# Two blocks of a transformer on one core: small loads on the load queue, their tables made later, joint units held through both halves, first loads in another order

## The chip, the core and the metric

The kernel runs on one core of one Trainium2 chip. A core has TensorE (PE, matrix products), VectorE (DVE), ScalarE (ACT), GpSimd (POOL) and SyncE (SP, which here only starts transfers), a scratchpad that all of them read and write, accumulator banks, and 16 DMA engines that bring data from HBM. Each engine works through its own queue in order and waits where an instruction needs another engine's result. The metric is the device time of one execution, in microseconds.

## What is computed

Two blocks, one after the other, on 256 tokens of width 1024, in float32. The first has a modulated mixer over the tokens x and a context ctx (attention beside a retention that runs in both directions) and a gated FFN; the second has an FFN, a gated recurrence (HGRN) beside a short convolution, cross-attention to a memory mem_2, and another FFN. Of the reference, what the change touches:

```python
mod_x = silu(c) @ w_mod + b_mod              # six vectors of 1024; columns 0 and 1: shift and scale
hx = rms_norm(x, g_pre_mix) * (1 + sc_m) + sh_m       # hc: the same of ctx, with c_ctx
qa, ka, va, qr, kr, vr, gr = split(h @ w_in)          # of hx and of hc
qa, ka = rms_norm(heads(qa), q_norm_g), rms_norm(heads(ka), k_norm_g)
lg = -exp(ret_decay)                         # per head; decays exp(lg * position) in the retention
ret_x = bidir_retention(rope(qr_x), rope(kr_x), vr_x, lg_f, lg_b, states of ctx)
...
z = rms_norm(x) @ w_in_2                     # HGRN f, q, i, g and the convolution's c, u, b
k_mem, v_mem = split(rms_norm(mem_2) @ w_kv_mem_2)
x = x + attention(x @ w_q_mem_2, k_mem, v_mem) @ w_o_mem_2
```

## The kernel before, in words

Products are made from float32 numbers in two parts: a high part `hi` that TensorE multiplies at its fast float32 rate, and the rest `lo`; a product is hi·hi plus hi·lo plus lo·hi (`mm3`). Tokens stand in tiles of 128: A and B of x, C and D of ctx.

Weights come in units of 128 x 1024 floats (512 KB). `Unit.load` (L386) starts the transfer on SyncE's queue into one of four raw buffers. `Unit.prepare` (L408) splits the unit: ScalarE copies the raw buffer to `hi`, VectorE subtracts to get `lo`, each in one of six ring slots, and the raw buffer comes free. `Unit.get` (L421) hands the unit to the matmuls; at the call that brings its count `uses` to 0 the ring slots go back to the list of free ones, and the next split may be written into the program for them. That split then waits on the chip until the last matmul that reads the slot is done.

The program is fixed when it is built. Threads (written as generators, such as `memory`, `projections`, `small_tables`, `joints`) yield what they need next; a planner picks one after the other and puts the loads and splits in between. What it picks sets the order of the instructions on each engine, and each engine keeps to that order on the chip. The loads stand in the sequence that the string `ORDER` (L40) spells: u is a unit of w_kv_mem_2, 0 and 1 are blocks of w_mod for its first two columns (these may lie in ring slots, unsplit), x is a tile of ctx or x (C, D, A, B), k, a, r, y, q, g are units of w_in, o of w_out, m the other blocks of w_mod, f a place in the first FFN.

At the start TensorE multiplies the w_kv_mem units with the normalised memory (`mm<-k,hi` in the trace) and the w_mod blocks with silu(c) (`acc<-...,cwide`) as they come in. When the sixteen blocks of columns 0 and 1 are done, ctx and x are modulated (`xj`) and the k, a, r projections follow.

`keep` holds the identity (its first 128 columns, loaded first of all) and constants: cosines, sines, positions. `small` holds q_norm_g, k_norm_g and the sixteen decays. Both feed `small_tables` (L948): ScalarE makes exp of the decays (`lg`), GpSimd multiplies it with positions (`dec`) and makes tables for the rotation (`rope`), then ScalarE takes the exponential of `dec`.

The joint stage multiplies w_in_2 units of 8 x 128 x 128 with both token tiles at once. `joint` (L1504) takes two units, each in two halves of 12 matmuls with a yield ahead of each half, so that other threads' work can come between. Between them run the level pairs of the recurrence (`hgrn`, L1564): two groups of small matmuls (`mm<-k,k`), whose results VectorE merges into `macc` with masked copies (`COPY_PREDICATED`).

Of the kernel before, what the change touches and what calls it, by code (L numbers as in the profile page):

```python
# [18 lines left out]
P = 128  # L19
# [17 lines left out]
SOFT2 = 4  # L37


ORDER = "1u11xux11ux11ux1u00u00u00u00ukukaaaaururrrymymymmyummmmmqmqmmmmmuqmqggggmmoooomomommmomouufmfmffmfmmfffffm"  # L40


COLS = {}
# [9 lines left out]
ROWS = {}  # L53
# [13 lines left out]
NKEEP = K_POS + 8  # L67
# [199 lines left out]
def blocks_kernel(ctx: ExitStack, tc: tile.TileContext, a, out):  # L267
    nc = tc.nc
    model = Model()
# [5 lines left out]
    def load(queue, out, in_):  # L275

        n = free_size(out) / 1024.0
        run = 4 * in_.shape[-1]
        model.op("dma", (1.21 + 281.0 / run) * n, (out,), (), 2.0)
        queue.dma_start(out=out, in_=in_)  # L280
# [51 lines left out]
    def pacc(shape=(P, 512)):  # L332
        return new(ps, "acc", shape)


    keep = const.tile([P, NKEEP], F32, name="keep")
    cols = const.tile([P, NCOL], F32, name="cols")
    small = const.tile([P, 144], F32, name="small")
# [142 lines left out]
    def w_unit(w, r0, kt, c0, width, uses, kind="split", early=False):  # L481
        src = w[r0:r0 + kt * P, c0:c0 + width].rearrange("(k p) c -> p k c", p=P)
        return Unit((kt, width), [(0, width, src)], uses, kind, early=early)
# [55 lines left out]
    def until(cond):  # L539
        if not cond():  # L540
            yield cond, None
# [98 lines left out]
    w_in2 = a["w_in_2"][0]  # L640
    accs = {}
    done = set()
# [17 lines left out]
    def load_x(t):  # L660
        def consume(u):
            done.add(("x", t))
        i = "ABCD".index(t)
        src = a["x"] if t in "AB" else a["ctx"]
        u = Unit(None, [], 1, consume)

        def load_it():
            x_in[t] = x_res[t] if t in "AB" else k4()
            load(nc.sync, x_in[t], src[0, (i % 2) * P:(i % 2 + 1) * P, :])
            u.there = model.ready(x_in[t])  # L670
        u.load = load_it

    mods = [(j, kt) for j in (2, 3, 4, 5) for kt in range(8)]

    units = {z: [] for z in "u01karyqgo"}

    def first(z):
        i = len(units.get(z, ()))
        if z == "m":
            if mods:  # L680
                mod_unit(*mods.pop(0))
            return
        if z == "x":
            if xs_left:
                load_x(xs_left.pop(0))
            return
        if z == "u":
            u = w_unit(wkv, 0, 8, (D + i * P) % (2 * D), P, 1)
        elif z in "01":
            u = w_unit(w_mod, i * P, 1, int(z) * D, D, 1, "plain", early=True)  # L690
        elif z == "k":
            u = w_unit(w_in, 512 * i, 4, 512, 256, 4)
        elif z == "o":

            u = w_unit(w_out, P * i, 1, 0, D, 2) if i >= 4 else Unit((1, D), [
                (0, D, w_out[64 * h:64 * h + 64, :].unsqueeze(1), slice(64 * g, 64 * g + 64))
                for g, h in enumerate((i, 4 + i))], 2)
        else:
            c0, uses = {"a": (0, 2), "r": (1280, 4), "y": (1792, 4), "q": (768, 2), "g": (2304, 2)}[z]
            u = w_unit(w_in, 256 * i, 2, c0, 512, uses)  # L700
        units[z].append(u)

    xs_left = list("CDAB")
    head, tail = ORDER.split("f", 1)
    for z in head:
# [49 lines left out]
        return Ffn(len(ffns), gu, dn, step)  # L755

    def units2(c0):
        return [[w_unit(w_in2, 0, 8, c0 + 256 * i + P * b, P, 1) for b in range(2)] for i in range(2)]

    f0 = ffn_units([(a["w_ffn_in"][0], 0), (a["w_ffn_in"][0], FF)], a["w_ffn_out"][0], tail)  # L760
    f1 = ffn_units([(a["ffn1_gate_2"][0], 0), (a["ffn1_up_2"][0], 0)], a["ffn1_down_2"][0])
# [12 lines left out]
    for i in range(2):  # L774
        for h in range(2):
            s = slice(h * 512, (h + 1) * 512)
# [9 lines left out]
    xt, xsT = {}, {}  # L786
# [3 lines left out]
    for i in range(2):  # L790
        for b in (0, 1):
            c = slice(i * P, (i + 1) * P)
            split_cols(mh[b][:, :, c], ml[b][:, :, c], "mem_norm_2", t_bank(mem_t[i], 4 * b), 0, 4 * b)

    load(nc.scalar, keep[:, P:NKEEP], a["consts"][:, P:NKEEP])
    o0 = ROWS["q_norm_g"][0]
    load(nc.scalar, small, a["rows"][o0:o0 + 144].partition_broadcast(P))

    def memory():

# [145 lines left out]
    lb = const.tile([P, 3, 4], F32, name="lb")  # L946

    def small_tables():  # L948
        yield (small, keep), None
        act(out=lg, in_=small[:, 128:144], func=ACTF.Exp)  # L950
        pool.tensor_scalar(out=lg, in0=lg, scalar1=-1.0, scalar2=None, op0=ALU.mult)
        for i in range(8):
            half = 0 if i in (0, 1, 4, 5) else 8
            pool.tensor_scalar(out=dec[:, i, :], in0=lg[:, half:half + 8], scalar1=keep[:, K_POS + i:K_POS + i + 1],
                               scalar2=None, op0=ALU.mult)
        e = sm(8)
        l0, l1 = (cols[:, COLS["lb_param_2"] + 4 * i:COLS["lb_param_2"] + 4 * i + 4] for i in range(2))
        dve.tensor_tensor(out=lb[:, 0, :], in0=l0, in1=l1, op=ALU.max)
        dve.tensor_tensor(out=e[:, 0:4], in0=l0, in1=lb[:, 0, :], op=ALU.subtract)
        dve.tensor_tensor(out=e[:, 4:8], in0=l1, in1=lb[:, 0, :], op=ALU.subtract)  # L960
        for i in range(2):
            cos = keep[:, K_COS + 64 * i:K_COS + 64 * i + 64]
            sin = keep[:, K_SIN + 64 * i:K_SIN + 64 * i + 64]
            for q in range(2):
                g = small[:, 64 * q:64 * q + 64]
                pool.tensor_tensor(out=rope[:, q, i, 0, :], in0=cos, in1=g, op=ALU.mult)
                pool.tensor_tensor(out=rope[:, q, i, 1, 0:32], in0=sin[:, 0:32], in1=g[:, 32:64], op=ALU.mult)
                pool.tensor_tensor(out=rope[:, q, i, 1, 32:64], in0=sin[:, 32:64], in1=g[:, 0:32], op=ALU.mult)
            pool.tensor_scalar(out=rope[:, 2, i, 0, :], in0=cos, scalar1=0.125, scalar2=None, op0=ALU.mult)
            pool.tensor_scalar(out=rope[:, 2, i, 1, :], in0=sin, scalar1=0.125, scalar2=None, op0=ALU.mult)  # L970
        yield from until(lambda: "C" in xsT)
        act(out=e, in_=e, func=ACTF.Exp)
        act(out=dec, in_=dec, func=ACTF.Exp)
        dve.tensor_scalar(out=dec[:, 4:8, :], in0=dec[:, 4:8, :], scalar1=0.125, scalar2=None, op0=ALU.mult)
        dve.tensor_tensor(out=lb[:, 2, :], in0=e[:, 0:4], in1=e[:, 4:8], op=ALU.add)
        dve.reciprocal(out=lb[:, 2, :], in_=lb[:, 2, :])
        dve.tensor_tensor(out=lb[:, 0, :], in0=e[:, 0:4], in1=lb[:, 2, :], op=ALU.mult)
        dve.tensor_scalar(out=lb[:, 1, :], in0=lb[:, 0, :], scalar1=-1.0, scalar2=1.0, op0=ALU.mult, op1=ALU.add)
# [525 lines left out]
    def joint(us):  # L1504

        yield "acc", None
        o = pacc((P, 2, 256))
        for b, u in enumerate(us):
            for half in range(2):
                yield xj, u  # L1510
                if half == 0:
                    hi, lo = u.get()
                for k in range(4 * half, 4 * half + 4):
                    mm3(o[:, b, :], hi[:, k, :], lo[:, k, :], xj[0][:, :, k, :], xj[1][:, :, k, :], k == 0, k == 7)
        st["o"] = o
# [257 lines left out]
```

## Time and profile before

| | us |
|---|---|
| median of three runs | 1071.71 (1069.2 to 1075.77) |
| the profiled execution | 1070.85 |
| its span in the trace | 1069.0 |
| TensorE busy | 1015.5 (95%) |
| VectorE busy | 691.3 (65%) |
| ScalarE busy | 517.0 (48%) |
| GpSimd busy | 11.2 (1%) |

Times in the trace count from the start of the span. A row of a timeline has a start, a length, the engine, the line that issued the instruction (L231, L258, L263 and L280 are helpers), the operation with output and input, how many in a row it merges, and in brackets how long the engine stood idle before and on whose result it waited. `PEclk` is the clock granted to TensorE, 1.00 being full speed.

### The profile page before, as it was taken

Reading aid. Unit: us, or ns where it says so; the run is one execution under the profiler, and the core shown is the slowest. Engines: PE = TensorE matmul, PEld = TensorE weight load, DVE = VectorE, ACT = ScalarE, POOL = GpSimd, SP = SyncE. Lnnn points to the kernel's source line nnn. Section 1 sums busy time; section 2 is a strip of 40 time slices with the busy share of each in tenths; the row PEclk is TensorE's granted clock in tenths of the full one; section 3 lists DMA queues with packets and bytes.
Section 4 is the critical chain, followed back from the end, with each engine's and each line's share of the span. In section 5 each row is a group of like instructions: output and inputs, shape, how many; then the busy total and the mean of one; then the engine's idle time right before and its main releaser. Section 6 shows DMA issues by size and latency. Waiting matters only on the chain. (4 is left out here: it accounts for less than half of the span.)

```text
span 1069.0 us, 16569 instructions
## 1 busy us (share of the span) xinstructions
PE 1015.5 (95%) x6506; PEld 891.1 (83%) x6506; DVE 691.3 (65%) x1140; ACT 517.0 (48%) x839; POOL 11.2 (1%) x34
## 2 busy tenths in 40 slices
PE   5989999998899999989999999998999999999996
PEld 3778877876699999968999998798978779999995
DVE  3468777787765655577656665667877476666654
ACT  5665245563654444445444444662245474444433
POOL 3000000000000000000000000000000000000000
PEclk9899999998899999999999999999999999999999
DMA  9863566562476766674566665574335256666641
GB/s 322 280 206 111 184 229 198 148 197 79 138 226 189 239 193 179 202 230 139 177 185 195 190 189 169 153 217 131 111 127 177 61 177 197 192 188 190 180 158 40
DMA packets 196110, 189.58 MB, mean 177 GB/s; under 512 B 6336, under 2 KB 167616, under 8 KB 196032
## 3 DMA queue, kind: packets, MB, share of 16 engines
q1 hardware_dynamic: 194160, 184.12, 56.3%
q10 hardware_dynamic: 1872, 4.41, 1.3%
q8 instruction: 51, 0.84, 0.3%
q14 instruction: 27, 0.22, 0.1%
HBM read 187.45 MB, written 1.05 MB: 176 GB/s over the span
## 5 line engine op out<-in xcount | busy, mean ns | idle before, releaser
L231 DVE TENSOR_TENSOR lo<-raw,hi 128x1024 fp32r<-128x1024 f32 x296 | 357.5, 1223 | 186.7 <-ACT hi L231 185.5
L231 ACT ACTIVATE hi<-raw 128x1024 fp32r<-128x1024 f32 x296 | 307.3, 1055 | 205.7 <-PE acc L258 88.9
L258 PE MATMUL mm<-xj,hi 128*128 128x256 f32 x1728 | 310.1, 282 | 0.0
L258 PEld LDWEIGHTS mm<-xj,hi 128*128 128x128 f32 x1728 | 268.6, 188 | 4.5
L258 PE MATMUL mm<-xj,lo 128*128 128x256 f32 x864 | 243.0, 281 | 0.0
L258 PE MATMUL acc<-hi,kh 128*128 128x512 f32 x528 | 176.4, 395 | 0.8 <-ACT kh L231 0.8
L258 PEld LDWEIGHTS mm<-xj,lo 128*128 128x128 f32 x864 | 162.6, 188 | 0.0
L258 PEld LDWEIGHTS acc<-hi,kh 128*128 128x128 f32 x528 | 99.1, 188 | 22.2 <-ACT kh L231 1.2
L258 PE MATMUL acc<-hi,k 128*128 128x512 f32 (+1 forms) x320 | 103.7, 394 | 4.7 <-DVE k L231 4.3
L258 PE MATMUL acc<-lo,kh 128*128 128x512 f32 x264 | 103.8, 393 | 0.0
L258 PE MATMUL acc<-hi,xj 128*128 128x512 f32 (+1 forms) x288 | 91.6, 389 | 1.7 <-DVE xj L231 1.7
L231 ACT ACTIVATE k<-k 128x256 f32<-128x256 f32 (+3 forms) x50 | 25.5, 510 | 108.4 <-DVE k L231 108.4
L258 PEld LDWEIGHTS acc<-hi,k 128*128 128x128 f32 x320 | 59.9, 191 | 19.5 <-issue 5.6
L258 PE MATMUL mm<-hi,xj 128*128 128x512 f32 x192 | 68.3, 420 | 3.0 <-ACT xj L231 2.7
L258 PEld LDWEIGHTS acc<-hi,xj 128*128 128x128 f32 x288 | 53.1, 188 | 14.5 <-DVE xj L231 2.3
L258 PE MATMUL acc<-lo,k 128*128 128x512 f32 (+1 forms) x160 | 61.6, 385 | 0.0
L263 PE MATMUL tp<-keep,k 128*128 128x128 f32 x288 | 46.8, 291 | 13.3 <-DVE k L231 4.3
L263 PEld LDWEIGHTS tp<-keep,k 128*128 128x128 f32 x288 | 35.3, 148 | 27.6 <-DVE k L231 7.6
L258 PE MATMUL acc<-xj,hi 128*128 128x256 f32 x320 | 58.2, 284 | 0.0
L258 PEld LDWEIGHTS acc<-lo,kh 128*128 128x128 f32 x264 | 49.8, 189 | 9.1
L258 PE MATMUL mm<-k,hi 128*128 128x256 f32 x256 | 52.6, 306 | 3.4 <-ACT hi L231 3.4
L258 PE MATMUL acc<-lo,xj 128*128 128x512 f32 (+1 forms) x144 | 54.9, 381 | 0.0
(161 smaller groups left out, 1152.1 us busy)
## 6 DMA issues: line engine op xcount, KB each, us to landing
raw<-in_w_in_dram SPq DMA_DIRECT2D x50, 512.0 KB, 4.6
raw<-in_ffn_down_dram SPq DMA_DIRECT2D x44, 512.0 KB, 3.7
raw<-in_w_ffn_in_dram SPq DMA_DIRECT2D x36, 512.0 KB, 4.8
raw<-in_ffn_gate_dram SPq DMA_DIRECT2D x36, 512.0 KB, 4.7
raw<-in_ffn_up_dram SPq DMA_DIRECT2D x36, 512.0 KB, 4.8
raw<-in_w_mod_dram SPq DMA_DIRECT2D x35, 512.0 KB, 4.5
raw<-in_w_ffn_out_dram SPq DMA_DIRECT2D x22, 512.0 KB, 4.2
raw<-in_w_kv_mem_dram SPq DMA_DIRECT2D x16, 512.0 KB, 4.9
```

The source lines that it names most:

```text
L231: return f(**kw)
L258: self.pe.matmul(out=out, lhsT=lhsT, rhs=rhs, start=start, stop=stop)
L263: self.pe.transpose(out, in_, ident)
```

## The change

The string ORDER is another one, with a new letter s. The loads of the rest of `keep` (132 KB) and of `small` (72 KB) move from ScalarE's queue, where they stood after the split of mem_2, to SyncE's, where they are a unit of their own (`load_small`) at the place of s. `small_tables` starts once these have been taken up and tile C of ctx has been transposed. Joint units have two uses instead of one and `get` is called for each half, so their ring slots go back after the second.

```diff
-ORDER = "1u11xux11ux11ux1u00u00u00u00ukukaaaaururrrymymymmyummmmmqmqmmmmmuqmqggggmmoooomomommmomouufmfmffmfmmfffffm"
+ORDER = "11uu1xux111usx11xu00u0uu00u00u0uaakakraurrrmyymmmyyummmmmquqmmmmmmgqqomggmgoommoommmomomuoufmfmffmfmmfffffm"
...
+    def load_small():
+        u = Unit(None, [], 1, lambda u: done.add(("x", "small")))
+
+        def load_it():
+            load(nc.sync, keep[:, P:NKEEP], a["consts"][:, P:NKEEP])
+            o0 = ROWS["q_norm_g"][0]
+            load(nc.sync, small, a["rows"][o0:o0 + 144].partition_broadcast(P))
+            u.there = model.ready(small)
+        u.load = load_it
...
+        if z == "s":
+            load_small()
+            return
...
     def units2(c0):
-        return [[w_unit(w_in2, 0, 8, c0 + 256 * i + P * b, P, 1) for b in range(2)] for i in range(2)]
+        return [[w_unit(w_in2, 0, 8, c0 + 256 * i + P * b, P, 2) for b in range(2)] for i in range(2)]
...
-    load(nc.scalar, keep[:, P:NKEEP], a["consts"][:, P:NKEEP])
-    o0 = ROWS["q_norm_g"][0]
-    load(nc.scalar, small, a["rows"][o0:o0 + 144].partition_broadcast(P))
...
     def small_tables():
-        yield (small, keep), None
+        yield from until(lambda: ("x", "small") in done and "C" in xsT)
...
-        yield from until(lambda: "C" in xsT)
         act(out=e, in_=e, func=ACTF.Exp)
         act(out=dec, in_=dec, func=ACTF.Exp)
...
             for half in range(2):
                 yield xj, u
-                if half == 0:
-                    hi, lo = u.get()
+                hi, lo = u.get()
```

In the program, first ScalarE's queue right after the split of mem_2, before (raw_158 and raw_166 are the first two w_kv_mem units, k_1_80 and k_2_81 mem_2, k_16 and k_18 ctx):

```order
L280 DMA keep<-in_consts_dram 128x264 [waits DMAHW2_49]
L280 DMA small<-in_rows_dram 128x144 [waits DMAHW3_49]
L231 ACT_TABLE_LOAD
L231 ACTIVATE lg<-small 128x16 [waits DMAHW3_49]
L231 ACTIVATE hi_221<-raw_158 128x1024 [waits DMAHW7_49]
L231 ACTIVATE k_37_265,sm_97<-k_1_80 128x1024
L231 ACTIVATE k_38_267,sm_97<-k_2_81 128x1024 [waits DMAHW5_49,DMAHW4_49]
```

and after, where raw_158 and raw_160 are the first two units:

```order
L231 ACTIVATE hi_199<-raw_158 128x1024 [waits DMAHW0_49]
L231 ACTIVATE hi_206<-raw_160 128x1024 [waits DMAHW1_49]
L231 ACTIVATE k_40_239,sm_97<-k_1_80 128x1024 [waits DMAHW3_49,DMAHW2_49]
L231 ACTIVATE k_41_241,sm_97<-k_2_81 128x1024 [waits DMAHW5_49,DMAHW4_49]
L231 ACTIVATE hi_255<-raw_166 128x1024 [waits DMAHW6_49,DMAHW4_49,PE_49]
L231 ACTIVATE k_48_261,sm_183<-k_17_164 128x1024 [waits DMAHW3_49]
L231 ACTIVATE k_49_267,sm_183<-k_19_168 128x1024 [waits DMAHW5_49]
```

Two loads, a table load and lg are gone from ahead of the first split, and the splits of the first two units stand one behind the other.

The same queue further on, around the exponential of dec, before (tp are transposed tiles, vm the memory's values on their way to the scratchpad, raw_225 a w_kv_mem unit):

```order
L231 ACTIVATE k_61_359<-k_18_168,sm_292 128x1024
L231 ACTIVATE sm_193<-sm_193 128x8
L231 ACTIVATE dec<-dec 128x64 [waits Pool_49]
L231 ACTIVATE vm<-tp_373,sm_270 128x128 [waits PE_49]
L231 ACTIVATE vm<-tp_373,sm_270 128x128
L231 ACTIVATE hi_413<-raw_225 128x1024 [waits DMAHW5_49,Activation_49]
```

and after, where raw_204 is the fifth w_kv_mem unit:

```order
L231 ACTIVATE k_65_365<-k_19_168,sm_270 128x1024
L231 ACT_TABLE_LOAD
L231 ACTIVATE lg<-small 128x16 [waits DMAHW3_49]
L231 ACTIVATE sm_378<-sm_378 128x8 [waits DVE_49]
L231 ACTIVATE dec<-dec 128x64 [waits Pool_49]
L231 ACTIVATE vm<-tp_411,sm_244 128x128 [waits PE_49]
L231 ACTIVATE vm<-tp_411,sm_244 128x128
L231 ACTIVATE k_66_367<-tp_451 128x512 [waits PE_49,Activation_49]
L231 ACTIVATE hi_457<-raw_204 128x1024 [waits DMAHW0_49]
```

The table load and lg now stand directly ahead of dec, which waits for GpSimd's work on lg; two copies to vm, one to k and the split of raw_204 follow.

ScalarE's queue in the joint stage, around the load of macc that comes shortly before the first level pair, before (hi<-raw are splits of units, k<-acc copies of joint results):

```order
L231 ACTIVATE hi_7206<-raw_7082 128x1024 [waits DMAHW4_49,DVE_49,PE_49]
L231 ACTIVATE hi_7236<-raw_7112 128x1024 [waits DMAHW5_49,DVE_49,PE_49]
L231 ACTIVATE k_1348_6999<-acc_7193 128x512 [waits PE_49]
L280 DMA macc_7258<-in_consts_dram 128x896
L231 ACTIVATE hi_7276<-raw_7147 128x1024 [waits DMAHW6_49,DVE_49,PE_49]
L231 ACTIVATE hi_7319<-raw_7177 128x1024 [waits DMAHW7_49,DVE_49,PE_49]
L231 ACTIVATE k_1377_7256<-acc_7263 128x512 [waits PE_49]
L231 ACTIVATE hi_7367<-raw_7210 128x1024 [waits DMAHW0_49,DVE_49,PE_49]
```

and after:

```order
L231 ACTIVATE hi_7200<-raw_7076 128x1024 [waits DMAHW3_49,DVE_49]
L231 ACTIVATE hi_7218<-raw_7094 128x1024 [waits DMAHW4_49,DVE_49,PE_49]
L231 ACTIVATE k_1348_6999<-acc_7187 128x512 [waits PE_49]
L231 ACTIVATE hi_7252<-raw_7141 128x1024 [waits DMAHW5_49,DVE_49]
L280 DMA macc_7258<-in_consts_dram 128x896
L231 ACTIVATE hi_7301<-raw_7159 128x1024 [waits DMAHW6_49,DVE_49,PE_49]
L231 ACTIVATE k_1374_7250<-acc_7263 128x512 [waits PE_49]
L231 ACTIVATE hi_7361<-raw_7204 128x1024 [waits DMAHW7_49,DVE_49]
L231 ACTIVATE hi_7379<-raw_7222 128x1024 [waits DMAHW0_49,DVE_49,PE_49]
```

Every split there waited for TensorE (PE) before; now every second one doesn't, among them the one ahead of the load of macc that stands next to the first level pair, and the copies of joint results fall at other places between them.

On SyncE's queue the fifth w_kv_mem load is now followed by two w_mod blocks that go to raw buffers, and five further w_kv_mem loads stand between these and the last w_mod block of columns 0 and 1. On TensorE eight w_kv_mem units and the sixteen blocks stand ahead of the end of the last block before and after; behind it stand two units before and three after, then the k projections. From the first FFN to the joint stage TensorE's order is the same. In VectorE's queue two subtractions instead of one now stand ahead of the masked copies of the third level pair, and one fewer ahead of the last chain of the recurrence.

## Rows read from the trace of the kernel before

**Rows 1.** The page: span, and busy time of each engine.

```profile
span 1069.0 us, 16569 instructions
...
PE 1015.5 (95%) x6506; PEld 891.1 (83%) x6506; DVE 691.3 (65%) x1140; ACT 517.0 (48%) x839; POOL 11.2 (1%) x34
```

**Rows 2.** Stretches: length, busy us (count) per engine, granted clock, DMA share, GB/s.

```profile
0.00:20.00 20.00, 8.75 (x45) 4.58 (x46) 6.02 (x21) 10.21 (x25) 3.35 (x12) 1.00 0.89 307
20.00:40.00 20.00, 17.62 (x120) 15.13 (x120) 8.18 (x29) 10.26 (x20) 5.09 (x20) 0.83 0.98 336
40.00:60.00 20.00, 18.37 (x171) 15.40 (x171) 8.13 (x22) 13.39 (x24) 0.00 (x0) 1.00 0.61 196
100.00:120.00 20.00, 20.00 (x113) 17.36 (x113) 18.01 (x32) 6.16 (x7) 0.00 (x0) 1.00 0.54 175
720.00:740.00 20.00, 17.38 (x146) 17.01 (x145) 13.00 (x17) 5.21 (x6) 0.00 (x0) 1.00 0.48 145
```

**Rows 3.** Timeline of ScalarE at the start: start, us, instruction [idle before <- releaser].

```profile
10.03 0.44 ACTq L280 DMA_DIRECT2D small<-in_rows_dram  x1
...
16.91 0.22 ACT L231 ACTIVATE lg<-small 128x16 f32<-128x16 f32 x1 [4.83 <-DMA small<-in_rows_dram]
17.04 1.04 ACT L231 ACTIVATE hi<-raw 128x1024 fp32r<-128x1024 f32 x1
```

**Rows 4.** Timeline of TensorE at the start.

```profile
12.33 1.08 PE L258 MATMUL acc<-lo,cwide 128*32 128x256 f32 x8 [1.71 <-DMA lo<-in_w_mod_dram]
...
18.13 0.80 PE L258 MATMUL mm<-k,hi 128*128 128x256 f32 x2 [3.43 <-ACT hi L231]
...
27.38 0.58 PE L258 MATMUL mm<-k,lo 128*128 128x256 f32 x1 [2.38 <-DVE lo L231]
```

**Rows 5.** Two stretches: the second w_kv_mem unit, and the k projections.

```profile
24.50:32.40 7.90, 5.52 (x29) 5.32 (x26) 3.92 (x19) 2.09 (x2) 0.59 (x2) 0.64 1.08 356
75.50:91.50 16.00, 13.09 (x99) 11.87 (x98) 13.47 (x33) 11.38 (x27) 0.00 (x0) 1.00 0.35 99
```

**Rows 6.** Timeline of ScalarE, joint stage.

```profile
725.82 1.06 ACT L231 ACTIVATE hi<-raw 128x1024 fp32r<-128x1024 f32 x1 [4.12 <-PE acc L258]
```

**Rows 7.** Timeline of VectorE, joint stage and its end.

```profile
726.91 1.23 DVE L231 TENSOR_TENSOR lo<-raw,hi 128x1024 fp32r<-128x1024 f32 x1 [4.11 <-ACT hi L231]
728.05 1.34 DVE L231 COPY_PREDICATED macc<-keep,mm 128x512 f32<-128x512 uint32 x2
...
775.92 1.23 DVE L231 TENSOR_TENSOR lo<-raw,hi 128x1024 fp32r<-128x1024 f32 x1 [1.82 <-ACT hi L231]
```

**Rows 8.** Timeline of TensorE, joint stage and its end.

```profile
730.64 2.02 PE L258 MATMUL mm<-k,k 128*128 128x128 f32 x16 [1.86 <-DVE k L231]
...
783.09 0.66 PE L263 MATMUL tp<-keep,k 128*128 128x128 f32 x4 [1.32 <-DVE k L231]
```

**Rows 9.** Timeline of GpSimd at the start.

```profile
17.57 3.35 POOL L231 TENSOR_SCALAR dec<-lg,keep 128x8 f32<-128x8 f32 x8
```

**Rows 10.** Timeline of ScalarE, 30 to 40 us.

```profile
35.58 0.24 ACT L231 ACTIVATE dec<-dec 128x64 f32<-128x64 f32 x1
```

**Rows 11.** Timeline of ScalarE at a table load in the joint stage.

```profile
704.13 1.28 ACT L231 ACT_TABLE_LOAD   x1
705.43 0.60 ACT L231 ACTIVATE k<-acc 128x512 f32<-128x512 f32 x1
```

**Rows 12.** Timeline of TensorE, 60 to 95 us.

```profile
64.55 0.64 PE L258 MATMUL acc<-raw,cwide 128*32 128x256 f32 x8
...
78.39 0.51 PE L258 MATMUL acc<-hi,xj 128*128 128x256 f32 x2 [1.11 <-DVE xj L231]
```

**Rows 13.** Timeline of SyncE's queue: issue, us, load.

```profile
3.54 0.43 SPq L280 DMA_DIRECT2D raw<-in_w_kv_mem_dram  x1
...
40.10 0.38 SPq L280 DMA_DIRECT2D raw<-in_w_kv_mem_dram  x1
...
47.82 0.38 SPq L280 DMA_DIRECT2D raw<-in_w_kv_mem_dram  x1
```

## The prediction

> **What bounds the kernel now.** I read the page first, then the table of stretches, then the rows of single engines at the two places that the change touches. TensorE is busy 1015.5 us of a span of 1069.0 [rows 1], so whatever the change brings must come out of 53.5 us in which TensorE stands still, and out of stretches in which it runs below its upper clock. The stretches show where that is [rows 2]: 11.25 us of the first 20 have no matmul, the next 20 lose 2.4 us and run at a granted clock of 0.83, and 720 to 740 us loses 2.6. From 100 to 120 us it is full (20.00 of 20.00); a unit that moves there costs its own length and nothing else.
>
> The start. ScalarE's queue runs in order. It issues the load of `small` at 10.03 us, and then its first exponential waits 4.83 us for it, until 16.91 [rows 3]. Right behind stands the split of the first w_kv_mem unit (17.04, 1.04 us), and TensorE takes up that unit at 18.13 after 3.43 us that the row puts down to this split [rows 4]. The second unit waits another 2.38 us at 27.38 for VectorE's half of its split [rows 4], and the stretch around it has a granted clock of 0.64, a mean between the chip's levels of 1.2 and 2.4 GHz [rows 5].
>
> The joint stage. A joint unit has two halves with a scheduling point between them. In the kernel before its ring slot was handed on after the first, so the next split was queued while the second half still read the slot. The rows show the price: ScalarE stands 4.12 us until 725.82 for TensorE, VectorE's subtraction waits 4.11 us behind that, and the masked copy of the first level pair stands behind it, at 728.05 [rows 6, 7]. TensorE then waits 1.86 us at 730.64 for the chain behind the copy, and 1.32 us at 783.09 for a chain that a subtraction with a wait of 1.82 us delayed [rows 7, 8].
>
> **Part 1, first split no longer behind `small`.** The change takes two DMAs and the exponential out of ScalarE's queue there. The first unit then waits for its own load. In the new order that load is the third large one behind mem_2; in the kernel before the third was the low half of w_mod, for which TensorE waited until 12.33 [rows 4]. With 1.04 us for the split [rows 3] the unit starts at about 13.4 instead of 18.13: **-4.7 us**; bounds -0.9, if only the issue time of two such DMAs (0.44 each) [rows 3] is saved, and -5.8 (18.13 less 12.33).
>
> **Part 2, the second unit's wait.** Its load now stands directly behind the first unit's, and its split directly behind the first split. The 2.38 us should go [rows 4]. Were the stretch also at the upper clock, 5.52 busy us times 0.36 would be another 2.0 [rows 5]. I take **-2.4**, bounds 0 and -4.4; the clock I leave out, because the unit still follows a stretch with little work.
>
> **Part 3, the tables made later.** They now start once ctx C is transposed, which puts four things into ScalarE's busy stretch around 30 us: a table load (1.28 us), the exponential (0.22), and `dec`'s exponential, which waits for GpSimd. From `lg` at 16.91 to the end of GpSimd's `dec` rows, 17.57 plus 3.35, are 4.0 us [rows 3, 9]; in the kernel before `dec`'s exponential came at 35.58, when GpSimd had been done with it for 14.7 us [rows 10]. Now ScalarE stands there for that time less lg's own 0.22, some 3.8 us, and queued behind it are two vm copies, a k copy and the split of raw_204: TensorE waits for the split, and its transposes for the banks that the copies free. Bounds 0 (TensorE has other units in hand) and +5.1 (3.8 plus the table load, all on the path); I take **+2.0**, nearer the middle since two split units are then ahead.
>
> The table load by itself: the row at 704.13 is followed by ScalarE's next instruction at 705.43, 1.30 us later, without a gap [rows 11]. The Trainium skill (ScalarE: Activation LUTs, What ACT_TABLE_LOAD costs) gives about 1.28 us for the load and 1.38 more for a drain, 2.66 in all, for every switch; by that, an estimate from this page, the term would be 1.4 us dearer. The rows decide here: no drain is seen.
>
> **Part 4, the loads in another order.** Up to the last w_mod load of columns 0 and 1 the queue now carries two more units (512 KB each) and the small loads. At the 307 and 336 GB/s of the first two stretches [rows 2] some 17 MB are in by about 56 us, against 64.55 at which TensorE takes the last of these blocks [rows 12]. So bytes are not the limit, as long as SyncE isn't held by raw buffers (a rival). Work before that point is the same, eight w_kv_mem units and sixteen w_mod blocks, so parts 1 to 3 carry over: the last block ends near 60 instead of 65.2. Behind it three units instead of two stand ahead of the k projections. These take 16.00 us, of which TensorE is busy 13.09, with waits such as 1.11 us for VectorE's xj [rows 5, 12]. The third unit fills time of that kind, and is missing later where TensorE is full: **-2.0**, bounds 0 and -2.9. The other moved units (m, y, q, g, o) lie in full stretches; one new wait like the second unit's would cost 2.4: **+0.5**, bounds -0.5 and +2.4.
>
> **Part 5, joint units held through both halves.** The split ahead of the first level pair no longer names TensorE among its waits, so the 1.86 us goes [rows 8]. At the end one subtraction fewer stands ahead of the last chain, so part of the 1.32 goes too. Against that, at the third pair two subtractions stand in a row ahead of the masked copy. I take **-2.5**, bounds 0 and -3.2. Holding the slot longer costs no matmul: the hardware had to wait for the second half in either kernel (the 4.12 us) [rows 6], only what queues behind that wait differs.
>
> **Sum.** -4.7 - 2.4 + 2.0 - 2.0 + 0.5 - 2.5 = -9.1 us. The profiled execution took 1070.85 us (span 1069.0), 0.9 below the median of 1071.71; the sum gives 1061.75 for it and **1062.6** against the median. I write 1062.5.
>
> **Rivals.**
> *The start is bound by its loads.* DMA is at 0.89 and 0.98 in the first two stretches [rows 2]; moving small loads from one queue to another takes no byte away. Then part 1 is worth only its issue time, -0.9, part 2 nothing, and the sum is -0.9 + 2.0 - 2.0 + 0.5 - 2.5 = -2.9: **1069**. For it speaks that share; against it that ScalarE's wait is put down to `small` alone, not to the unit's load issued at 3.54 on the other queue [rows 3, 13]. The Trainium skill (DMA: Bandwidth & Descriptors, Issuing engines are not separate DMA queues) says that DMAs from any engine run on the same 16 DMA engines and interleave, so a second queue saves only the sequencer's time to start them; that is this rival's rule.
>
> *The joint wait only moves*, to the third pair with its two subtractions. Part 5 is then 0 and the sum -6.6: **1065**.
>
> *More than I take.* -4.7 - 4.4 + 0.5 - 2.9 - 3.2 with nothing for moved units, -14.7: **1057**. For it: full clock after an earlier start, and ScalarE's stall covered.
>
> *Slower: raw buffers hold SyncE.* Two w_mod blocks now lie in raw buffers behind raw_204, and five more w_kv_mem loads precede the last w_mod load, each waiting for one of the four buffers. In the kernel before such a cycle took 7.7 us (40.10 to 47.82) [rows 13]. If ScalarE's stall delays the splits, the buffers come free late, and each cycle makes TensorE wait like the second unit did: 2.4 us and 2.0 of clock, 4.4. Without part 2 the sum is -6.7, so from two such waits on it is slower than before, and with four it is +10.9: **1083**. Against it: in the kernel before those cycles show no such wait, since 40 to 60 us is busy 18.37 of 20 [rows 2].
>
> **How the numbers follow.** Chances: forecast 0.47 (1059 to 1066), loads 0.17, joint wait moved 0.10, more 0.18, slower 0.08. One per cent, about what a measurement of this kernel can tell from no change, is 10.7 us: faster by more is under 1061.0, which holds the case "more" and somewhat under half of the forecast, 0.18 + 0.22 = 0.40. Slower by more is the last rival, 0.08; the rest, 0.52, lies within. The range runs from 1055, below "more", to 1071, above the first rival; what is left out is the slower case and the tails of those two.
>
> **What would show it.** Right: the first w_kv_mem matmul at 13 to 14 us; no wait of the second unit; `dec`'s exponential with an idle time of 3 to 4 us put down to GpSimd; the last w_mod block of columns 0 and 1 ending near 60; k projections with under 2 us of idle time; no wait of TensorE before the first level pair, and under 0.7 us before the last chain. Wrong: SyncE rows 7 us apart between 30 and 55, granted clock under 0.8 there, or a wait over 1 us at the third level pair. My weakest term is part 3: whether TensorE has enough split units in hand while ScalarE stands.

## The result and the profile after

The changed kernel takes 1059.53 us (median of four runs, 1055.50 to 1061.01), the kernel before 1072.95 in the same comparison: ratio 0.9871, 95% interval 0.9829 to 0.9913, 13.4 us less. The forecast was 1062.5 us, within 1055 to 1071. In a later comparison the ratio was 0.9884 (0.9851 to 0.9918). A ratio is not formed as the quotient of the two medians, so the two can differ by some tenths of a per cent. The profiled execution took 1061.01 us, its span is 1059.2.

The page of after, to be read beside [rows 1]:

```profile
span 1059.2 us, 16575 instructions
...
PE 1011.6 (96%) x6506; PEld 889.1 (84%) x6506; DVE 691.4 (65%) x1140; ACT 517.8 (49%) x839; POOL 10.6 (1%) x34
```

TensorE's idle time fell from 53.5 to 47.6 us, its busy time by 3.9 (fewer matmuls at the lower clock and after waits). The table of stretches of after, beside [rows 2] and the second of [rows 5]; columns as there:

```profile
0.00:20.00 20.00, 12.01 (x65) 7.89 (x65) 7.57 (x21) 11.01 (x25) 0.66 (x6) 1.00 0.89 291
20.00:40.00 20.00, 18.63 (x174) 14.57 (x171) 10.09 (x38) 13.40 (x25) 7.79 (x25) 1.00 1.00 342
40.00:60.00 20.00, 15.34 (x116) 13.06 (x116) 8.11 (x17) 12.32 (x21) 0.00 (x0) 0.83 0.89 279
74.20:88.90 14.70, 12.98 (x99) 11.94 (x98) 12.07 (x31) 10.41 (x24) 0.00 (x0) 1.00 0.33 98
220.00:240.00 20.00, 19.38 (x127) 16.82 (x126) 15.14 (x33) 8.52 (x25) 0.00 (x0) 0.83 0.46 136
680.00:800.00 120.00, 120.00 (x848) 111.78 (x847) 93.33 (x157) 57.14 (x85) 0.00 (x0) 1.00 0.51 153
```

The first 20 us have 12.01 us of matmuls instead of 8.75, and 20 to 40 us runs at 1.00. But 40 to 60 us, which held 18.37 us before, holds 15.34 at a clock of 0.83. In 680 to 800 us TensorE never stands; before, it was busy 114.97 of the 120:

```profile
680.00:800.00 120.00, 114.97 (x818) 106.19 (x817) 84.91 (x135) 50.92 (x67) 0.00 (x0) 1.00 0.49 146
```

TensorE's timeline of after at the start:

```profile
14.09 0.79 PE L258 MATMUL mm<-k,hi 128*128 128x256 f32 x2 [1.81 <-ACT hi L231]
...
42.67 0.66 PE L263 MATMUL tp<-keep,k 128*128 128x128 f32 x4 [1.18 <-ACT vm L231]
46.80 1.08 PE L258 MATMUL acc<-lo,cwide 128*32 128x256 f32 x8 [3.48 <-DMA lo<-in_w_mod_dram]
...
64.63 0.67 PE L258 MATMUL tp<-k,ones 128*128 128x256 f32 x2 [1.62 <-DVE k L231]
```

The first w_kv_mem unit begins at 14.09 instead of 18.13, and nothing up to 42 us waits as long as the second unit did [rows 4]. Then a w_mod block is late by 3.48 us, and rows of two matmuls behind it, 0.40 long at the upper clock, take 0.63. The last block of columns 0 and 1 ends at 63.0 instead of 65.2, and the tp<-k,ones row behind it, the sums of the table below, starts 2.6 us earlier than this row of before:

```profile
67.24 0.78 PE L258 MATMUL tp<-k,ones 128*128 128x256 f32 x2 [2.05 <-DVE k L231]
```

That is within what profiles of one start differ by: kernels with the start of before have the row at 63.00 to 67.24, those with the start of after at 63.18 to 64.63 (the column of sums below).

ScalarE of after, around the exponential of dec (beside [rows 3, 10]):

```profile
29.98 1.28 ACT L231 ACT_TABLE_LOAD   x1
31.27 0.22 ACT L231 ACTIVATE lg<-small 128x16 f32<-128x16 f32 x1
...
34.27 0.26 ACT L231 ACTIVATE dec<-dec 128x64 f32<-128x64 f32 x1 [2.68 <-POOL dec L231]
...
35.41 1.06 ACT L231 ACTIVATE hi<-raw 128x1024 fp32r<-128x1024 f32 x1
```

It stands 2.68 us for GpSimd, and the split of the fifth unit is the row at 35.41. The Trainium skill's 1.38 us drain beside a table load (ScalarE: Activation LUTs, What ACT_TABLE_LOAD costs) is not there either: the instruction ahead of the load ends at 29.96, and 29.98 to 31.27 is 1.29 us. GpSimd's row (beside [rows 9]), and SyncE's queue (beside [rows 13]):

```profile
31.93 2.31 POOL L231 TENSOR_SCALAR dec<-lg,keep 128x8 f32<-128x8 f32 x8
```

```profile
30.08 2.95 SPq L280 DMA_DIRECT2D hi<-in_w_mod_dram  x1
37.76 1.91 SPq L280 DMA_DIRECT2D raw<-in_w_kv_mem_dram  x2
39.72 0.57 SPq L280 DMA_DIRECT2D lo<-in_w_mod_dram  x1
```

SyncE stands from 33.0 (30.08 plus 2.95) to 37.76, when the raw buffer of the fifth unit is free, and the load issued at 39.72 is the block for which TensorE waits at 46.80. The joint stage in TensorE's timeline, all eight pairs of small matmuls, beside [rows 8], and VectorE at the first of them, beside [rows 7]:

```profile
718.96 1.95 PE L258 MATMUL mm<-k,k 128*128 128x128 f32 x16
...
723.62 1.95 PE L258 MATMUL mm<-k,k 128*128 128x128 f32 x16
...
729.73 1.95 PE L258 MATMUL mm<-k,k 128*128 128x128 f32 x16
...
735.84 1.95 PE L258 MATMUL mm<-k,k 128*128 128x128 f32 x16
...
740.50 1.95 PE L258 MATMUL mm<-k,k 128*128 128x128 f32 x16
...
745.17 1.95 PE L258 MATMUL mm<-k,k 128*128 128x128 f32 x16
...
751.28 1.95 PE L258 MATMUL mm<-k,k 128*128 128x128 f32 x16
...
758.82 1.95 PE L258 MATMUL mm<-k,k 128*128 128x128 f32 x16
```

```profile
719.32 1.23 DVE L231 TENSOR_TENSOR lo<-raw,hi 128x1024 fp32r<-128x1024 f32 x1 [0.52 <-ACT hi L231]
720.46 1.34 DVE L231 COPY_PREDICATED macc<-keep,mm 128x512 f32<-128x512 uint32 x2
```

No pair waits. VectorE's subtraction ahead of the first masked copies waits 0.52 us where it waited 4.11.

### The profile page after: what moved, and what is told of

Read it like the earlier page. It is cut to its first block, busy times and chain, and to the rows that moved or that the text cites. A ratio compares the mean times of both kernels' runs of the same rounds, so it can differ in the third digit from the quotient of the medians.

```text
span 1059.2 us, 16575 instructions
## 1 busy us (share of the span) xinstructions
PE 1011.6 (96%) x6506; PEld 889.1 (84%) x6506; DVE 691.4 (65%) x1140; ACT 517.8 (49%) x839; POOL 10.6 (1%) x34
## 4 chain that ended last, share of the span: by engine, by line
PE 81%; DVE 7%; issue 4%; ACT 4%; DMA 3%; POOL 0%; SPq 0%; ACTq 0%; DVEq 0%; POOLq 0%
PE acc L258 39%; PE mm L258 39%; PE tp L263 3%; ACT k L231 2%; DVE sm L231 2%; DVE k L231 2%; DVE lo L231 2%; ACT hi L231 1%; DVE macc L231 1%; DMA raw<-in_w_ffn_out_dram 1%; DMA row<-in_rows_dram 1%; DMA lo<-in_w_mod_dram 1%; DMA raw<-in_w_in_dram 0%; DMA raw<-in_w_mod_dram 0%; DVE xj L231 0%
## 5 line engine op out<-in xcount | busy, mean ns | idle before, releaser
L231 ACT ACTIVATE hi<-raw 128x1024 fp32r<-128x1024 f32 x296 | 307.0, 1055 | 189.9 <-PE acc L258 65.7
L231 DVE TENSOR_TENSOR k<-k,k 128x256 f32<-128x256 f32 (+4 forms) x79 | 40.7, 524 | 21.6 <-ACT k L231 20.3
```

The costliest lines, as they stand in the source:

```text
L231: return f(**kw)
```

## The experiments

Each kernel is compared with the kernel before; ratios are with their 95% intervals. There were several such comparisons, each with its own runs of before (medians 1071 to 1074), so kernels of two comparisons are set against each other by their ratios, not by their medians. joint_only, no_joint, dec_after_D and after_again are one comparison; order_only, small_only, long_stall and early_lg another; the two hold kernels a third; the two mods_first kernels a fourth. The table gives starts of rows in each profile: the first w_kv_mem matmul, the sums behind the last w_mod block (tp<-k,ones), the first matmul of the first FFN (acc<-hi,kh), the first level pair (mm<-k,k), the product with macc (mm<-k,macc), and the stretch from the pair to macc.

| kernel | median us | ratio | unit 1 | sums | FFN | pair | macc | pair to macc |
|---|---|---|---|---|---|---|---|---|
| before | 1071 to 1074 | 1 | 18.13 | 67.24 | 298.33 | 721.49 | 774.70 | 53.21 |
| after, first profile | 1059.53 | 0.9871 (0.9829 to 0.9913) | 14.09 | 64.63 | 294.97 | 718.96 | 767.26 | 48.30 |
| after_again | 1059.17 | 0.9884 (0.9851 to 0.9918) | 13.31 | 63.57 | 291.39 | 714.99 | 763.25 | 48.26 |
| joint_only | 1064.14 | 0.9938 (0.9913 to 0.9963) | 16.94 | 63.87 | 294.50 | 720.18 | 768.44 | 48.26 |
| hold_beside_pairs | 1065.16 | 0.9943 (0.9915 to 0.9970) | 17.22 | 65.70 | 294.78 | 717.38 | 763.77 | 46.39 |
| hold_f_q | 1071.48 | 1.0015 (0.9988 to 1.0042) | 16.88 | 63.00 | 293.58 | 717.80 | 769.95 | 52.15 |
| no_joint | 1066.24 | 0.9926 (0.9903 to 0.9949) | 13.69 | 63.18 | 291.58 | 715.81 | 770.57 | 54.76 |
| order_only | 1070.60 | 0.9964 (0.9943 to 0.9985) | 18.12 | 63.47 | 302.00 | 726.27 | 779.48 | 53.21 |
| small_only | 1070.33 | 0.9968 (0.9948 to 0.9988) | 13.88 | 60.05 | 296.60 | 721.08 | 775.86 | 54.78 |
| dec_after_D | 1055.97 | 0.9850 (0.9822 to 0.9879) | 13.28 | 59.66 | 289.43 | 715.31 | 763.57 | 48.26 |
| long_stall | 1060.99 | 0.9875 (0.9850 to 0.9900) | 13.23 | 64.97 | 295.44 | 719.16 | 767.42 | 48.26 |
| early_lg | 1054.18 | 0.9819 (0.9794 to 0.9844) | 12.55 | 57.55 | 287.41 | 710.81 | 759.11 | 48.30 |
| mods_first | 1054.46 | 0.9845 (0.9811 to 0.9880) | 12.75 | 59.24 | 290.13 | 714.63 | 762.93 | 48.30 |
| early_lg_mods_first | 1052.96 | 0.9826 (0.9787 to 0.9865) | 13.62 | 57.07 | 284.21 | 711.90 | 760.16 | 48.26 |

A single profile holds the early columns only to some us: four kernels have the start of before (before, joint_only and the two hold kernels), and their FFN begins anywhere from 293.58 to 298.33; the profiled executions of the two hold kernels were the fastest of their 11 and 12. The last column is steadier. So the start is judged by ratios here, the joint stage by both.

**The joint part alone and left out.** joint_only:

```diff
+        ... w_unit(w_in2, 0, 8, c0 + 256 * i + P * b, P, 2) ...
-                if half == 0:
-                    hi, lo = u.get()
+                hi, lo = u.get()
```

> Only the joint units are held through both halves; loads, tables and their order are those of before. Theory (the joint part stands by itself): the joint stage's waits of TensorE vanish, so the gain is what the traces differ by there, 6.9 us (the lag of after behind before grows from -2.53 us ahead of the first level pair to -9.41 behind the last chain), ratio about 0.9936; the rows of the start stay as in before, first w_kv_mem matmul near 18 us. Rival (the joint stage gains because it begins at another time or with other loads in flight): under 3 us, ratio 0.997 or more, with waits of TensorE ahead of the level pairs left.

0.9938, and 48.26 us from pair to macc, without a wait: the joint part stands by itself. (By medians it gains 9.1 us, 1073.25 to 1064.14, by its ratio 6.6.) no_joint is the changed kernel with these lines as before.

> The changed kernel with the joint part undone: new order of loads, small loads on SyncE's queue, tables later. Theory: the joint stage has its waits back (1.86 us ahead of the first full level pair, 5 us of idle time in 680 to 800 us) and what is left is the start, 2.5 us as the profile of after shows it at the joint stage's begin, or 5.4 if the stretch at half clock near 226 to 233 us doesn't come in every execution: ratio 0.995 to 0.998. Rival: the start gives the larger part, 7 to 9 us, and the ratio is under 0.993.

0.9926, which is the rival's: the start gives 7 to 8 us (7.0 by medians, 1073.25 to 1066.24), above the upper end of what the theory allowed. The waits are back, as TensorE's timeline of no_joint shows at the first pairs:

```profile
717.18 1.60 PE L258 MATMUL mm<-k,k 128*128 128x128 f32 x12 [0.77 <-DVE k L231]
...
724.96 3.15 PE L258 MATMUL mm<-k,k 128*128 128x128 f32 x16 [1.90 <-DVE k L231]
```

The two gains, 6.6 and 7.9 us by ratios (0.0062 and 0.0074 of 1073), add to 14.5, against 12.4 and 13.8 for the whole in its two comparisons (0.0116 and 0.0129). Each has an interval of some 2.5 us either way, so this agrees, and nothing finer can be read from it.

**Which units.** `units2` gets the number of uses, `get` is called again if one is left:

```diff
+    u_zf, u_zq, u_zc, u_zu, u_zb = units2(512, 1), units2(0, 1), units2(2560, 2), units2(3072, 2), units2(2048, 2)
```

for hold_beside_pairs, and 2, 2, 1, 1, 1 for hold_f_q.

> The kernel before, with only the joint units that run beside the level pairs (the convolution's c, u and b, 12 units) held through both halves; f and q as before. Theory (TensorE waits because a split queued in the middle of a unit stands in VectorE's queue ahead of the level pairs' masked copies): nearly the whole joint gain, 4 to 6 us between the first level pair and the product with macc (before: 53.2 us, all units held: 48.3), ratio 0.994 to 0.997. Rival (the gain comes from where f and q end, so from the state in which the pairs begin): that stretch stays over 52 us, ratio 0.998 or more.

> The counterpart: only f and q held, the units beside the level pairs as before. Theory: the splits beside the pairs still wait in the middle of a unit, the stretch from the first level pair to the product with macc stays near 52 to 53 us, at most 1 to 2 us gained at the first pair, ratio 0.998 to 1.000. Rival: the stretch comes under 50 us, ratio 0.994 to 0.997.

0.9943 with 46.39 us, and 1.0015 with 52.15. (In hold_beside_pairs 252 joint matmuls stand in that stretch, in the others 276; 24 take 2.7 us, 723.62 less 718.96 less a pair's 1.95 in the rows of after, so 46.39 is the 48.26 without them and with one wait of 0.74 us.) TensorE's timeline of hold_f_q has a first pair without a wait, and then the waits of before:

```profile
717.80 1.95 PE L258 MATMUL mm<-k,k 128*128 128x128 f32 x16
...
725.92 2.02 PE L258 MATMUL mm<-k,k 128*128 128x128 f32 x16 [1.86 <-DVE k L231]
...
735.64 2.02 PE L258 MATMUL mm<-k,k 128*128 128x128 f32 x16 [0.18 <-DVE k L231]
...
761.50 2.02 PE L258 MATMUL mm<-k,k 128*128 128x128 f32 x16 [0.45 <-DVE k L231]
```

So it is the units beside the pairs: it is shown that holding them takes the waits away, and the f and q units, where a wait of 0.76 us went, give nothing that the ratio can tell. From the first pair to the end of the span the profiles say the same: 341.3 us in hold_beside_pairs (1058.7 less 717.38) and 346.4 in hold_f_q, against 347.5 before and 340.2 after.

**The start, one part at a time.** order_only has the new string without s, all else as before; small_only has the string of before with an s behind its twelfth letter, `load_small` and the later tables:

```diff
-ORDER = "1u11xux11ux1ux1u...
+ORDER = "1u11xux11ux1s1ux1u...
```

> Only the string of loads is the new one (without s): the small loads stay on ScalarE's queue, the tables are made at once, joint units are as before. Theory (the two parts of the start need each other): the first w_kv_mem unit still waits for the exponential of small and begins at 17 to 18 us, the second follows without its 2.4 us wait, the exponential of dec finds GpSimd done; 2 to 4 us are gained, ratio 0.996 to 0.998. Rival (the order of loads alone carries the start): the gain is that of the kernel without the joint part, ratio 0.991 to 0.994.

> The order of loads of before with an s after the same twelve letters, small loads on SyncE's queue, tables later; joint units as before. Theory: the first unit begins near 13 us, but the second waits longer, since its load and its split are no earlier than in before (lo near 26 us); a part of the 4 to 5 us goes there, and ScalarE stands some 2.7 us for GpSimd again; 1 to 4 us gained, ratio 0.996 to 0.999. Rival (the small loads alone carry the start): ratio 0.991 to 0.994.

0.9964 and 0.9968: each gives 3 to 4 us (with intervals of some 2 us either way), and together they give the 7 to 8 of no_joint. In order_only the first unit still begins at 18.12, behind small; in small_only at 13.88, and its second unit waits 0.70 us; the longer wait that I expected didn't come. That small_only gains more than the 0.9 us of issue time tells against the rival that only loads bound the start. The rule named there (the Trainium skill, DMA: Bandwidth & Descriptors, Issuing engines are not separate DMA queues) isn't touched by it: DMA's share in the first 20 us is 0.89 before and after, 0.92 in small_only; what went was an engine's wait in its own queue, not a transfer.

**ScalarE's wait for GpSimd.** dec_after_D puts the exponentials off:

```diff
+        yield from until(lambda: "D" in xsT)
         act(out=e, in_=e, func=ACTF.Exp)
         act(out=dec, in_=dec, func=ACTF.Exp)
```

> The changed kernel, with the exponentials of e and dec put off until tile D of ctx is transposed, so that ScalarE doesn't stand 2.7 us for GpSimd ahead of the split of the fifth w_kv_mem unit. Theory (that stand holds the split, so its raw buffer, so SyncE between 33 and 37.8 us, so the w_mod block for which TensorE waits 3.48 us at 46.8 and runs slowly after): the split comes near 32.5 instead of 35.4, SyncE goes on some 3 us earlier, the 3.48 us shrinks to about 0.5 and the last w_mod block of columns 0 and 1 ends near 60 instead of 63; about 3 us less than the changed kernel, ratio to before about 0.984. Rival (the loads themselves are the limit, DMA share is 1.00 in 20 to 40 us): the wait stays over 2.5 us wherever it stands and the ratio is that of the changed kernel within 0.001.

The median is 3.2 us under that of the changed kernel in the same comparison (1059.17), though the intervals of the two ratios overlap, and the sums come at 59.66. But the way there was another than I wrote. SyncE's queue of dec_after_D:

```profile
29.53 2.82 SPq L280 DMA_DIRECT2D hi<-in_w_mod_dram  x1
36.68 2.14 SPq L280 DMA_DIRECT2D raw<-in_w_kv_mem_dram  x2
38.87 0.57 SPq L280 DMA_DIRECT2D lo<-in_w_mod_dram  x1
```

and of after_again:

```profile
29.37 2.90 SPq L280 DMA_DIRECT2D hi<-in_w_mod_dram  x1
37.66 1.22 SPq L280 DMA_DIRECT2D raw<-in_w_kv_mem_dram  x2
38.93 0.82 SPq L280 DMA_DIRECT2D lo<-in_w_mod_dram  x1
```

The raw buffer is free 1 us earlier, not 3 (ScalarE next waits 1.77 us for a transpose instead), and the w_mod block is issued at the same time, 38.87 and 38.93. TensorE, dec_after_D first, then after_again:

```profile
43.42 0.44 PE L263 MATMUL tp<-keep,k 128*128 128x128 f32 x2 [0.81 <-ACT vm L231]
43.62 0.48 PE L258 MATMUL mm<-k,hi 128*128 128x256 f32 x2
...
49.14 0.64 PE L258 MATMUL acc<-lo,cwide 128*32 128x256 f32 x8
```

```profile
42.60 0.66 PE L263 MATMUL tp<-keep,k 128*128 128x128 f32 x4 [1.23 <-ACT vm L231]
46.21 1.08 PE L258 MATMUL acc<-lo,cwide 128*32 128x256 f32 x8 [2.96 <-DMA lo<-in_w_mod_dram]
```

With the exponentials elsewhere the planner put a whole w_kv_mem unit (43.62 to 48.39) ahead of the late block, and the block has come when TensorE gets to it. long_stall lengthens the wait by moving GpSimd's eight `dec` instructions behind the rotation tables:

> The changed kernel with GpSimd's work in another order: the rotation tables first, then dec, so that ScalarE's exponential of dec waits for GpSimd some 5.3 us longer (about 8 us), with the same work. Theory (that stand costs TensorE through the split of the fifth unit and the raw buffers): the split comes at 40 to 41 us instead of 35.4, SyncE's next w_kv_mem load 4 to 5 us later, TensorE's waits between 35 and 55 us grow by 3 to 6 us and the k projections begin that much later; 3 to 6 us slower than the changed kernel, ratio to before 0.990 to 0.994. Rival (TensorE has enough units, or loads are the limit): within 1 us of the changed kernel, 0.986 to 0.989.

ScalarE stood 6.72 us instead of 2.67, SyncE's next w_kv_mem load came at 41.19 instead of 37.66, as expected; but in 30 to 55 us TensorE stood only 2.0 us longer (17.78 us busy; 19.74 in after_again), the k projections begin at 74.54 instead of 73.14, and 0.9875 is not to be told from 0.9884. The theory that this stand sets the time, through the split and the raw buffer, falls in its size: four more us of it cost 1.4 us between these two profiles (the first profile of after has the k projections at 74.21) and nothing that the ratios can tell.

**Which load is behind which.** mods_first moves two w_mod loads ahead of the two w_kv_mem loads that need raw buffers:

```diff
-ORDER = "11uu1xux111usx11xu00u0uu00u00u0u...
+ORDER = "11uu1xux111usx11xu00u000uuu00u0u...
```

> The changed kernel with two w_mod loads moved ahead of two w_kv_mem loads in the string (u000uu for u0uu00 behind the two blocks in raw buffers), tables as in the changed kernel. In its trace SyncE stands until 37.7 us for the raw buffer that the split of the fifth unit frees, and the w_mod block for which TensorE waits 3 us at 46 us is issued behind that, at 38.9. Theory (it is this place behind a load that needs a raw buffer that makes the block late): the two blocks are issued by 35 us, the wait of 3 us for w_mod goes, the last block of columns 0 and 1 ends 2 to 4 us earlier; ratio to before 0.984 to 0.987. Rival (16 DMA engines are full there, so another order only makes the w_kv_mem units late): a wait of the same 2 to 3 us for a split stands in its place, ratio 0.987 to 0.990.

The two are issued by 32.8 (31.81 and 32.37), TensorE's longest wait for a w_mod block behind 30 us is 0.90, the sums come at 59.24, and ScalarE still stands 2.66 us for GpSimd. The wait for a split that the rival had in its place isn't there. By the ratios (0.9845 and 0.9884) that is some 4 us under after_again, but the intervals overlap, so the gain is likely and not settled. early_lg starts lg and GpSimd as soon as small is there and leaves the wait for tile C to the exponentials; early_lg_mods_first does both:

```diff
-        yield from until(lambda: ("x", "small") in done and "C" in xsT)
+        yield from until(lambda: ("x", "small") in done)
...
+        yield from until(lambda: "C" in xsT)
         act(out=e, in_=e, func=ACTF.Exp)
```

> The changed kernel with the exponential of lg and GpSimd's work started as soon as the small loads are there, and only the exponentials of e and dec after tile C. Theory: lg stands two copies and one normalisation earlier, GpSimd has 2 to 3 us more, ScalarE's wait ahead of dec is under 1 us and the split of the fifth unit 2 to 3 us earlier; 1 to 3 us under the changed kernel, as with dec put off, ratio 0.984 to 0.987. Rival: lg waits for the landing of small itself (issued at 21 us) and the stand only moves ahead, ratio 0.988 or more.

> Both: lg and GpSimd's work started as soon as the small loads are there, and the two w_mod loads moved ahead. With lg early alone TensorE had no wait over 1.1 us behind 13 us, ratio 0.982. Theory: nothing is left there that the moved loads could save, ratio 0.980 to 0.984. Rival: the two gains add, ratio under 0.980; or the w_kv_mem units come late, ratio over 0.985.

0.9819 for early_lg, more than expected: ScalarE's wait is 0.67, the late block again has a unit ahead of it, and the sums come at 57.55. Its interval (0.9794 to 0.9844) lies below that of after_again (0.9851 to 0.9918) and overlaps that of after's first comparison (0.9829 to 0.9913): it beats the kernel before clearly and the changed kernel very likely. With the loads moved as well it is 0.9826; the two don't add, as the theory had it, and can't be told apart. TensorE's stretch of that kernel, to be read beside the third row of after above:

```profile
40.00:60.00 20.00, 18.00 (x167) 14.98 (x160) 12.40 (x23) 14.90 (x26) 0.00 (x0) 1.00 1.02 315
```

It is 18.00 us busy at full clock, where the changed kernel had 15.34 at 0.83.

## Why the prediction was right in sum, and which term was mis-sized

The time moved as forecast, 13.4 us for 9.1; of the 4.3 us that were missing, 4.1 are part 5's, by joint_only's ratio. Point by point:

**Part 1** (-4.7). The first unit begins at 14.09, 4.0 earlier, and at 12.55 to 13.88 in the other kernels without small ahead of it. Right in mechanism and size (other executions of before's start begin it at 16.88 to 17.22, so the gain is some 3 to 5 us); small_only shows that it is this move. One reading was off: the row lo<-in_w_mod is not the low half of w_mod but a whole block of it, unsplit, in a ring slot named lo. It changes nothing in the sum.

**Part 2** (-2.4). The second unit has no wait, where the four kernels with the start of before wait 2.38, 2.38, 2.39 and 2.38 us for it: right. The clock that was left out (2.0) can't be called gained, though after shows 20 to 40 us at 1.00: with the start of before that stretch is at 0.83, 1.00, 0.91 and 0.98 in the four profiles, so at most a part of those 2.0 us is the change's, and the profiles can't say how much.

**Part 3** (+2.0). The place was right: ScalarE stands for GpSimd with the split of the fifth unit behind it, 2.68 us instead of 3.8, since the eight `dec` instructions took 2.31 us and not 3.35. The price came by another way. TensorE's loss, 3.48 us and the slow unit behind it, belongs to a w_mod block whose load stands behind a w_kv_mem load without a raw buffer; mods_first keeps the stand and has no such wait, long_stall lengthens the stand and loses little more. I had this wait in my "slower" rival (SyncE's rows 7 us apart: 30.08 to 37.76), and it came once, not four times. So the +2.0 stands for a mechanism other than the one it was worked out from, and that the start's sum fits is in part luck.

**Part 4** (-2.0 and +0.5). The k projections take 14.70 us with 1.72 idle instead of 16.00 with 2.91: -1.2. That is more than a profile's scatter: 14.8 us from their first row to the first acc<-lo,k of 128x512 in three profiles of after's start, 16.2 to 16.8 in four of before's. The last w_mod block was to end near 60; it ended at 63.0, 2.2 us earlier than before and not 5, behind the late block. The whole start is 7 to 8 us by no_joint, where my parts 1 to 4 sum to -6.6.

**Part 5** (-2.5) is the term that was mis-sized: joint_only gives 6.6 us. I counted the two longest waits, 1.86 and 1.32 [rows 8], and took off a part for a wait that might move to the third pair. In fact all seven waits went, 5.03 us in 680 to 800 us (114.97 to 120.00 busy). The five that neither I nor [rows 8] counted, in before:

```profile
722.86 1.60 PE L258 MATMUL mm<-k,k 128*128 128x128 f32 x12 [0.76 <-DVE k L231]
...
740.39 2.02 PE L258 MATMUL mm<-k,k 128*128 128x128 f32 x16 [0.18 <-DVE k L231]
...
750.10 2.02 PE L258 MATMUL mm<-k,k 128*128 128x128 f32 x16 [0.20 <-DVE k L231]
...
758.08 2.02 PE L258 MATMUL mm<-k,k 128*128 128x128 f32 x16 [0.26 <-DVE k L231]
...
766.24 2.02 PE L258 MATMUL mm<-k,k 128*128 128x128 f32 x16 [0.44 <-DVE k L231]
```

With them went the slower first matmuls behind each wait (2.02 for a pair after a wait, 1.95 without) and a loss that no idle time shows: in after a joint row of 0.29 us starts at 723.50 and the pair at 723.62, 0.17 us before that row ends, which a pair that waits can't do; for seven waits that is an estimate of 1.2 us. The bound of -3.2 was no bound, because it left out every wait under 1 us; the row of the whole stretch would have given 5. The rival that the wait moves to the third pair fell: two subtractions stand ahead of that pair's masked copies in VectorE's queue (728.63 and 730.90, the copies at 732.04), and neither the pair (729.73) nor the next one (735.84) waits.

Of the rivals, the one on loads fell with small_only, the slower one showed itself once, and "more than I take" (1057) came as near to 1059.5 as the forecast, for another reason than it named.

The stretch of after at 220 to 240 us with a clock of 0.83 belongs to that execution: its six matmuls mm<-xj,k took 2.04 us there and 1.10 in after_again, behind a wait of about the same length. The other profiles have either as well, 2.04 in long_stall, 1.40 in small_only and 1.10 in the rest:

```profile
226.39 2.04 PE L258 MATMUL mm<-xj,k 64*128 64x256 f32 x6 [0.62 <-DVE k L231]
```

```profile
225.12 1.10 PE L258 MATMUL mm<-xj,k 64*128 64x256 f32 x6 [0.72 <-DVE k L231]
```

Its lead over before falls there from 5.4 us (214.33 against 219.76 at the first such matmul) to 2.4 (234.32 against 236.72 at the last group); it is one reason why the first profile shows the start smaller than the ratios do.

Open: what ScalarE's stand costs by itself. Both changes that shorten it (dec_after_D and early_lg) also put a unit ahead of the late block on TensorE; a kernel with the same order and no stand wasn't tried. Open too is where in the trace the start's 7 to 8 us lie: the ratios carry them, while the profiles of one start differ by up to 4.8 us at the first FFN.

## What to carry to other kernels

Count a removed wait with all its kin: take the idle time of the whole stretch from the table of windows, not the two longest rows. Where engines run in a fixed order, don't queue work on a buffer that is still being read: the wait itself is hidden, but not what stands behind it, and the same holds for a load without a free buffer ahead of one that has its place. And where a planner orders the engines, an edit that takes a wait away also moves other work: look at both orders before the gain is put down to the wait.

## Not expected

GpSimd's eight `dec` instructions took 3.35 us before [rows 9] and 2.31 after, with nothing in them changed; the other kernels that run them at 16 to 22 us took 3.35 too, or 4.40 (order_only), and those that run them behind 28 us 2.29 to 2.31. Why is open. Four kernels with the same instructions and order up to the first FFN reach it between 293.58 and 298.33 us, so one profile of each side could not have sized the start.
